# Modulation columns in TensorE column groups, GpSimd low halves at the entry of the down projection, token-order copies placed behind the gates' sigmoids

## The chip, the cores and the metric

The kernel runs on one core of one Trainium2 chip. The metric is the device time of one execution in microseconds (us). The kernel before takes 1423.31 us, the median of 3 runs (1421.92 to 1427.57).

## The reference

One layer over 1024 latent tokens of width 1024, with a prefix of 256 context tokens, in float32:

```
sh1, sc1, g1, sh2, sc2, g2 = split(silu(c) @ mod_w + mod_b, 6)        # one row each, 1024 wide
csh1, csc1, ...            = split(silu(c_ctx) @ mod_w + mod_b, 6)
h  = rmsnorm(x,   norm1_g) * (1 + sc1)  + sh1
hc = rmsnorm(ctx, norm1_g) * (1 + csc1) + csh1
p  = h @ w_in                            # 512 S5 inputs, 3 x 512 short convolution, 2 x 1024 gates
pc = hc @ w_in[:, :512]
y_a = s5_branch(p[:512], pc, ...)        # two directions, state handed from ctx, gelu, then a GLU
y_b = b_gate * conv1d(c_gate * x_val)
merged = sigmoid(p gate_a) * (y_a @ proj_a) + sigmoid(p gate_b) * (y_b @ proj_b)
x  = x + g1 * (merged @ w_out)
h2 = rmsnorm(x, norm2_g) * (1 + sc2) + sh2
a, v = split(depthwise_conv3x3(h2 @ w_up))          # 2 x 2816 channels on a 16 x 64 grid
x  = x + g2 * ((silu(a) * v) @ w_down)
out = rmsnorm(x, final_g)
```

The first two lines are the modulation; the change rewrites how sh1, sc1, csh1 and csc1 are computed.

## The kernel before

Every float32 product of the layer is made of three passes of TensorE over values split into a high half (a rounded copy, written by ScalarE) and a low half (the difference, written by VectorE or GpSimd): `mm3` (L211 to L214) issues high by high, low by high, and high by low. `weight` (L190 to L204) loads 128 rows of a weight and splits them (`whi`, `wlo`); `split` (L206 to L208) does it for an activation.

A tile scheduler sets, at build time, the order of the instructions of each engine from the data dependences, the buffer counts of the pools and its own cost estimates; the engines then take them strictly in that order. `tc.issue_after(ins)` puts what is written inside it behind an instruction. SyncE (SP) and ScalarE (ACT) issue the loads, also in order.

The stages that the change touches, in order of time:

- The start (0 to 62 us). Four tiles of x are loaded and normalised (`norm_rows`: squares summed by ScalarE, a short chain of VectorE operations for the inverse root, four products). For each of 8 slices k of the width, a column of (1 + scale) * norm1_g (`A1`) and one of the shift (`B1`) are needed; `transpose_mod` turns the slice of x, ScalarE applies both columns (`h32a`, L302) and copies the high half (`hhi`, L304), VectorE makes the low half (`hlo`, L307), and `u_pass` multiplies by the slice's w_in rows (`mm_ua`, 12 matmuls per k, accumulated over k). `mod_scale` (L344 to L360) gets the scale columns by TensorE: 8 float32 products with the two condition columns as the stationary operand, a row of two by 128 that ScalarE copies, and a transpose. `mod_shift` (L362 to L374) gets the shift columns by VectorE: a dot product of a 128 x 1024 tile of mod_w transposed with a row of silu(c) that `cond_rows` spread over the partitions by 16 transposes and four copies. `mod_shift` also loads and splits the w_in slice (`wuh`, `wul`, L373).
- The second half of the tokens and the context (63 to 115 us), then the S5 tables, the convolution, the scan and its readouts (to about 400 us), with projections in between. A readout `Zt` goes through memory (`Zd`), and `z` is read back and put into token order by ScalarE (L862). Next to it the gates run: `gate` (L831 to L835) multiplies, then ScalarE's sigmoid (`sggb`) empties the accumulator `mm_gb`.
- The output projection (590 to 700 us): `mixed` (L965 to L971) splits the merged activations into `mh` and `ml`.
- The gated MLP's up projection with its 3 x 3 convolution (700 to 1169 us): `up_conv` (L1047 to L1067). Of the nine taps, ScalarE does the centre and one vertical neighbour (`side`, added by GpSimd, L1056), VectorE does seven (L1064). There are 22 pairs of column tiles; `f[k]` is the product of a pair.
- The down projection in two groups of four token tiles (1169 to 1414 us): `down_operands` (L1092 to L1099) loads w_down's rows and splits `f[k]` into `fhd`, `fld`. In the first group the first four k take token tiles 0 and 1 first, because the accumulators of tiles 2 and 3 are still read by the last convolutions.

Of the kernel before, what the change touches and what calls it, by code (L numbers as in the profile page):

```python
# [42 lines left out]
NAT = KT  # L43
# [113 lines left out]
def layer_kernel(es: ExitStack, tc, I, out):  # L157
# [68 lines left out]
    modx = const.tile([P, 16], F32, name="modx")  # L226
# [35 lines left out]
    mp = pool("mp", bufs=5, stack=es_a)  # L262
# [22 lines left out]
    def norm_rows(xt, ntile, key, dst, tpool, eng, junk=None):  # L285
# [3 lines left out]
        for i in range(ntile):  # L289
            sq = act.activation(junk, xt[i], AF.Square, accum_out=ss[:, i:i + 1])  # L290
# [32 lines left out]
    sc1 = cond_rows(0, mp)
    sx = cond_rows(1, mp)
# [13 lines left out]
    mj = mp.tile([P, D], BF16, name="mj", bufs=1)  # L338

    def mod_dot(mw, s_, dst, junk=mj):  # L340
        dve.tensor_tensor_reduce(out=junk, in0=mw, in1=s_, scale=1.0, scalar=0.0, op0=ALU.mult, op1=ALU.add,
                                 accum_out=dst)

# [880 lines left out]
```

## Time and profile before

| | |
|---|---|
| time, median of 3 runs | 1423.31 us (1421.92 to 1427.57) |
| the profiled execution | 1423.9 us |
| its span, first to last instruction | 1422.0 us |
| granted TensorE clock, mean | 0.997 of full speed |
| busy share: TensorE, VectorE, ScalarE, GpSimd | 97%, 68%, 37%, 29% |
| data moved | 148.71 MB |

The trace has one line for every instruction, in microseconds from the span's start. PE is TensorE's matmuls, PEld its weight loads, DVE is VectorE, ACT is ScalarE, POOL is GpSimd, SP is SyncE. L is the line of the kernel. "out<-in" are the kernel's names; a square bracket at a row's end gives how long the engine stood idle before it, and what ended that. Consecutive instructions of one kind are merged in a row; the duration is then that of all. The duration of a matmul overlaps with the next one's, so the step between two starts is what one costs.

### The profile page before, as it was taken

Reading aid. Unit: us, or ns where it says so; the run is one execution under the profiler, and the core shown is the slowest. Engines: PE = TensorE matmul, PEld = TensorE weight load, DVE = VectorE, ACT = ScalarE, POOL = GpSimd, SP = SyncE. Lnnn points to the kernel's source line nnn. Section 1 sums busy time; section 2 is a strip of 40 time slices with the busy share of each in tenths; the row PEclk is TensorE's granted clock in tenths of the full one; section 3 lists DMA queues with packets and bytes.
Section 4 is the critical chain, followed back from the end, with each engine's and each line's share of the span. In section 5 each row is a group of like instructions: output and inputs, shape, how many; then the busy total and the mean of one; then the engine's idle time right before and its main releaser. Section 6 shows DMA issues by size and latency. Waiting matters only on the chain.

```text
span 1422.0 us, 16940 instructions
## 1 busy us (share of the span) xinstructions
PE 1385.7 (97%) x6488; PEld 1136.4 (80%) x6488; DVE 971.4 (68%) x1464; ACT 528.0 (37%) x749; POOL 406.8 (29%) x183
## 2 busy tenths in 40 slices
PE   7999999999999999999999999999999999999997
PEld 4788887788878888788888888888888887888886
DVE  6866779998336751376487788778878887338655
ACT  5643862212653312244343233332332342324322
POOL 0000000002011133520056545555555465623002
PEclk9999999999999999999999999999999999999999
DMA  9613212512867562242111111111111115433421
GB/s 329 212 54 97 68 60 89 139 52 90 245 219 199 184 203 60 74 148 90 51 60 46 58 45 45 52 52 45 45 58 47 45 59 187 139 102 136 147 90 60
DMA packets 80401, 148.71 MB, mean 105 GB/s; under 512 B 22208, under 2 KB 47040, under 8 KB 80320
## 3 DMA queue, kind: packets, MB, share of 16 engines
q1 hardware_dynamic: 74848, 128.46, 28.9%
q10 hardware_dynamic: 5472, 19.17, 4.0%
q8 instruction: 51, 0.84, 0.2%
q14 instruction: 30, 0.25, 0.1%
HBM read 129.80 MB, written 19.90 MB: 105 GB/s over the span
## 4 chain that ended last, share of the span: by engine, by line
PE 86%; DVE 5%; ACT 3%; DMA 3%; issue 1%; POOL 0%; SPq 0%; ACTq 0%; POOLq 0%; DVEq 0%
PE mm_up L214 11%; PE mm_up L212 11%; PE mm_up L213 11%; PE mm_dn L213 5%; PE mm_dn L212 5%; PE mm_dn L214 5%; PE mm_o L214 2%; PE mm_o L212 2%; PE mm_ga L214 2%; PE mm_o L213 2%; PE mm_ga L213 2%; PE mm_ga L212 2%; PE mm_gb L212 1%; PE mm_gb L213 1%; PE mm_gb L214 1%
## 5 line engine op out<-in xcount | busy, mean ns | idle before, releaser
L1064 DVE SCALAR_TENSOR_TENSOR acc<-mm_up,cw,acc 128x945 f32<-128x945 f32 (+2 forms) x308 | 375.0, 1222 | 100.3 <-POOL acc L1056 91.6
L203 POOL TENSOR_TENSOR wlo<-raw,whi 128x1024 fp32r<-128x1024 f32 x80 | 197.8, 2474 | 705.0 <-ACT whi L200 704.9
L200 ACT ACTIVATE whi<-raw 128x1024 fp32r<-128x1024 f32 x126 | 133.5, 1060 | 530.7 <-issue 165.3
L214 PE MATMUL mm_up<-h2hi,wlo 128*128 128x512 f32 x704 | 273.9, 389 | 0.5 <-POOL wlo L203 0.5
L212 PE MATMUL mm_up<-h2hi,whi 128*128 128x512 f32 x704 | 273.5, 389 | 0.4 <-DVE h2hi L999 0.4
L213 PE MATMUL mm_up<-h2lo,whi 128*128 128x512 f32 x704 | 273.9, 389 | 0.0
L214 PEld LDWEIGHTS mm_up<-h2hi,wlo 128*128 128x128 f32 x704 | 132.1, 188 | 28.3 <-POOL wlo L203 0.9
L212 PEld LDWEIGHTS mm_up<-h2hi,whi 128*128 128x128 f32 x704 | 132.1, 188 | 27.9 <-DVE h2hi L999 0.7
L213 PEld LDWEIGHTS mm_up<-h2lo,whi 128*128 128x128 f32 x704 | 132.1, 188 | 27.7
L213 PE MATMUL mm_dn<-wlo,fhd 128*128 128x512 f32 x308 | 120.1, 390 | 2.5 <-POOL wlo L203 2.5
L212 PE MATMUL mm_dn<-whi,fhd 128*128 128x512 f32 x308 | 118.5, 389 | 1.5 <-DVE acc L1064 1.5
L214 PE MATMUL mm_dn<-whi,fld 128*128 128x512 f32 x308 | 119.9, 389 | 0.0
L1056 POOL TENSOR_TENSOR acc<-acc,side 128x960 f32<-128x960 f32 x44 | 100.4, 2283 | 0.0
L208 DVE TENSOR_TENSOR fld<-f,fhd 128x512 fp32r<-128x512 f32 x44 | 52.8, 1215 | 49.0 <-ACT fhd L207 49.0
L873 DVE CUSTOM_DVE_ANT_0 mw<-mw,sc 128x1024 f32<-128x1024 f32 x32 | 44.1, 1387 | 45.1 <-DMA mw<-in_mod_wT_dram 29.8
L213 PEld LDWEIGHTS mm_dn<-wlo,fhd 128*128 128x128 f32 x308 | 57.8, 188 | 15.3 <-POOL wlo L203 3.5
L212 PEld LDWEIGHTS mm_dn<-whi,fhd 128*128 128x128 f32 x308 | 57.8, 188 | 14.0 <-DVE acc L1064 1.9
L214 PEld LDWEIGHTS mm_dn<-whi,fld 128*128 128x128 f32 x308 | 57.8, 188 | 12.0
L203 DVE TENSOR_TENSOR wlo<-raw,whi 128x1024 fp32r<-128x1024 f32 x46 | 57.0, 1239 | 9.8 <-ACT whi L200 9.8
L1154 POOL TENSOR_TENSOR x1r<-x1r,fgb 128x512 f32<-128x512 f32 x16 | 21.7, 1362 | 129.6 <-ACT fjk L1153 129.6
L1075 POOL TENSOR_TENSOR f<-f,acc 128x1024 f32<-128x1024 f32 x22 | 53.3, 2424 | 10.0 <-DVE acc L1064 10.0
L197 DVE TENSOR_TENSOR raw<-raw,g2b 128x1024 f32<-128x1024 f32 x22 | 28.4, 1289 | 38.1 <-DMA raw<-in_ffn_w_down_dram 38.1
(325 smaller groups left out, 2667.1 us busy)
## 6 DMA issues: line engine op xcount, KB each, us to landing
raw<-in_ffn_w_up_dram SPq DMA_DIRECT2D x44, 512.0 KB
raw<-in_ffn_w_down_dram SPq DMA_DIRECT2D x44, 512.0 KB
mw<-in_mod_wT_dram SPq DMA_DIRECT2D x32, 512.0 KB
raw<-in_w_in_dram SPq DMA_DIRECT2D x17, 512.0 KB
wt<-Yd SPq DMA_DIRECT2D x16, 384.0 KB
raw<-in_w_in_dram ACTq DMA_DIRECT2D x11, 512.0 KB
mt<-in_mod_wT_dram SPq DMA_DIRECT2D x8, 512.0 KB
mn<-in_mod_nat_dram SPq DMA_DIRECT2D x8, 512.0 KB
```

The source lines that it names most:

```text
L197: dve.tensor_tensor(raw, raw, scale, op=ALU.mult)
L200: act.activation(hi, raw, AF.Copy)
L203: (lo_eng or dve).tensor_tensor(lo, raw, hi.bitcast(F32), op=ALU.subtract)
L208: return dve.tensor_tensor(lo, src, hi.bitcast(F32), op=ALU.subtract)
L212: pe.matmul(ps, lh, rh, start=first, stop=False)
L213: pe.matmul(ps, lh, rl, start=False, stop=False)
L214: pe.matmul(ps, ll, rh, start=False, stop=last)
L873: dve.tensor_tensor_reduce(out=mw, in0=mw, in1=sc2, scale=1.0, scalar=0.0, op0=ALU.mult, op1=ALU.add, accum_out=modc[:, n:n + 1])
L1056: pool_e.tensor_tensor(acc[:, 1:, :], acc[:, 1:, :], side[:, 1:, :], op=ALU.add)
L1064: dve.scalar_tensor_tensor(acc[:, r0:r1, c0:c1], u[:, r0 + dr:r1 + dr, c0 + dc:c1 + dc], cw[:, m, i:i + 1], acc[:, r0:r1, c0:c1], op0=ALU. ...
L1075: pool_e.tensor_tensor(f[k], f[k], v, op=ALU.mult)
L1154: pool_e.tensor_tensor(xt[i][:, sl], xt[i][:, sl], fgb[:, sl], op=ALU.mult)
```

## The change

- `mod_cols1` replaces `mod_scale` and the dots of `mod_shift`. All 16 column tiles (8 of shift, 8 of scale) go to TensorE. The two condition columns are padded with zeros to 32 (`condp`), and the eight partial products of a tile are written to four groups of 32 rows of the accumulator, two accumulated in each. ScalarE copies the 128 x 256 result of a k, and a product with a 0/1 matrix of two columns (`sel`) sums the four groups and turns the row into a column. ScalarE then writes `A1` and `B1` from the accumulator. `cond_rows`, its 16 transposes and four copies are gone, and so are the 16 dots.
- `load_wu` keeps the load and split of the w_in slice. The pool of modulation tiles has 7 buffers in place of 5; the tiles are the same size and number.
- The squares of x tiles 1 and 3 move from ScalarE to VectorE.
- The loads of the four readout tiles `zj` are written ahead of the modulation's, and the copies to token order (`z_tokens`) are to be issued behind a gate's sigmoid. silu(c) for the later modulation columns is a sigmoid by ScalarE and a product by VectorE.
- `mh` has three buffers in place of two.
- The last pair of the up projection takes its side tap on VectorE: no `side` copy and no GpSimd addition.
- The low halves of `f[0]` to `f[5]` for the first down group are made by GpSimd, behind the low half of the weight of that k.
- The deferred products of token tiles 2 and 3 are ordered by tile, then by k.

The diff, cut to its core:

```diff
--- before.py
+++ after.py
@@ -40,7 +40,7 @@
-NAT = KT
+NAT = 2 * KT
...
         with held("dve") if lo_eng is None else nullcontext():
-            (lo_eng or dve).tensor_tensor(lo, raw, hi.bitcast(F32), op=ALU.subtract)
+            hold["lo"] = (lo_eng or dve).tensor_tensor(lo, raw, hi.bitcast(F32), op=ALU.subtract)
         return hi, lo
 
-    def split(hi, lo, src):
+    def split(hi, lo, src, eng=None):
         act.activation(hi, src, AF.Copy)
-        return dve.tensor_tensor(lo, src, hi.bitcast(F32), op=ALU.subtract)
+        return (eng or dve).tensor_tensor(lo, src, hi.bitcast(F32), op=ALU.subtract)
 
     def mm3(ps, lhs, rhs, first, last):
         (lh, ll), (rh, rl) = lhs, rhs
...
-    mp = pool("mp", bufs=5, stack=es_a)
+    mp = pool("mp", bufs=7, stack=es_a)
...
-            sq = act.activation(junk, xt[i], AF.Square, accum_out=ss[:, i:i + 1])
+            if key == "a" and i % 2:
+                dve.tensor_tensor_reduce(out=tpool.tile([P, D], BF16, name=f"jd_{key}{i}", tag="h32"), in0=xt[i], in1=xt[i],
+                                         scale=1.0, scalar=0.0, op0=ALU.mult, op1=ALU.add, accum_out=ss[:, i:i + 1])
+            else:
+                sq = act.activation(junk, xt[i], AF.Square, accum_out=ss[:, i:i + 1])
...
-    act.activation(cond, cond, AF.Silu)
-
-
-    def cond_rows(i, mpool):
-        t = mpool.tile([P, D], F32, name=f"cr{i}", bufs=1)
-        for n in range(2):
-            ps = ax_tile([P, HALF], f"cr{i}_{n}")
-            for k in range(4):
-                pe.transpose(ps[:, k * P:(k + 1) * P], cond[:, 4 * n + k, i:i + 1].to_broadcast([P, P]), ident)
-            act.activation(t[:, n * HALF:(n + 1) * HALF], ps, AF.Copy)
-        return t
-
-    sc1 = cond_rows(0, mp)
-    sx = cond_rows(1, mp)
+    condp = mp.tile([P, KT, 32], F32, name="condp", bufs=1)
+    dve.memset(condp, 0.0)
+    act.activation(condp[:, :, 0:2], cond, AF.Silu)
+    sel = mp.tile([P, 2], F32, name="sel", bufs=1)
+    dve.tensor_tensor(sel, ident[:, 0:2], ident[:, 32:34], op=ALU.add)
+    for j in (64, 96):
+        dve.tensor_tensor(sel, sel, ident[:, j:j + 2], op=ALU.add)
+    modb1 = mp.tile([P, KT], F32, name="modb1", bufs=1)
+    dve.scalar_tensor_tensor(modb1, modb[:, KT:2 * KT], 1.0, n1g, op0=ALU.add, op1=ALU.mult)
...
-    def mod_scale(k):
-        n = KT + k
-        mw = mp.tile([P, D], F32, name=f"mn{k}", tag="mw")
-        dma[k] = sync.dma_start(mw, I["mod_nat"][k])
-        pr = prp.tile([P, P + 2], F32, name=f"pr{k}", tag="pr")
-        row, col = pr[0:2, :P], pr[:, P:]
-        for q in range(KT):
-            pe.matmul(row, cond[:, q, :], mw[:, q * P:(q + 1) * P], start=(q == 0), stop=(q == KT - 1))
-        rw = mp.tile([2, P], F32, name=f"rw{k}", tag="rw", bufs=1)
-        act.activation(rw, row, AF.Copy)
-        pe.transpose(col, rw, ident[0:2, 0:2])
-        dve.tensor_tensor(A1[:, :, k], col, modb[:, n:n + 1].to_broadcast([P, 2]), op=ALU.add)
-        dve.scalar_tensor_tensor(A1[:, :, k], A1[:, :, k], 1.0, n1g[:, k:k + 1].to_broadcast([P, 2]),
-                                 op0=ALU.add, op1=ALU.mult)
-
-    def mod_shift(k):
-        mw = mp.tile([P, D], F32, name=f"mt{k}", tag="mw")
-        sync.dma_start(mw, I["mod_wT"][k * P:(k + 1) * P, :])
+    def mod_cols1(k):
+
+
+        pr = prp.tile([P, 2 * P + 4], F32, name=f"pr{k}", tag="pr")
+        rows = pr[:, :2 * P].rearrange("p (c n) -> p c n", c=2)
+        cols = pr[:, 2 * P:].rearrange("p (c i) -> p c i", c=2)
+        for c in range(2):
+            mw = mp.tile([P, D], F32, name=f"m{c}_{k}", tag="mw")
+            dma[k] = sync.dma_start(mw, I["mod_nat"][c * KT + k])
+            for s_ in range(2):
+                for j in range(4):
+                    q = 4 * s_ + j
+                    pe.matmul(rows[32 * j:32 * j + 32, c, :], condp[:, q, :], mw[:, q * P:(q + 1) * P],
+                              start=(s_ == 0), stop=(s_ == 1))
+        rw = mp.tile([P, 2, P], F32, name=f"rw{k}", tag="rw", bufs=1)
+        act.activation(rw, rows, AF.Copy)
+        for c in range(2):
+            pe.matmul(cols[:, c, :], rw[:, c, :], sel, start=True, stop=True)
+        act.activation(B1[:, :, k], cols[:, 0, :], AF.Identity, bias=modb[:, k:k + 1])
+        act.activation(A1[:, :, k], cols[:, 1, :], AF.Identity, scale=n1g[:, k:k + 1], bias=modb1[:, k:k + 1])
+
+    def load_wu(k):
         raw = wp.tile([P, D], F32, name=f"wuraw{k}", tag="raw")
         junk[k] = raw[:, SW:].bitcast(BF16)
         sync.dma_start(raw[:, :SW].rearrange("p (m n) -> p m n", m=MS),
                        I["w_in"][0:MS].rearrange("m p (k n) -> k p m n", k=KT)[k])
         act.activation(wuh[k], raw[:, :SW], AF.Copy)
         with held("dve"):
-            mod_dot(mw, sc1, modc[:, k:k + 1])
-            dve.tensor_tensor(B1[:, 0, k:k + 1], modc[:, k:k + 1], modb[:, k:k + 1], op=ALU.add)
             dve.tensor_tensor(wul[k], raw[:, :SW], wuh[k].bitcast(F32), op=ALU.subtract)
-            mod_dot(mw, sx, modx[:, k:k + 1])
...
-    mod_shift(0)
     for k in range(NE):
-        mod_scale(k)
-    mod_shift(1)
+        mod_cols1(k)
+        load_wu(k)
     half_a(0)
     for k in range(KT):
-        if k + 2 < KT:
-            if k + 2 >= NE:
-                mod_scale(k + 2)
-            mod_shift(k + 2)
-        if k + 2 == XB:
+        if k + NE < KT:
+            mod_cols1(k + NE)
+            load_wu(k + NE)
+        if k + NE == XB:
...
-    dve.tensor_tensor(B1[:, 1, :], modx[:, :KT], modb[:, :KT], op=ALU.add)
...
-        act.activation(sg, psg, AF.Sigmoid)
+        hold["sig"] = act.activation(sg, psg, AF.Sigmoid)
...
+    zj = []
     for m in range(MS):
-        zj = zp.tile([P, L, NCL], F32, name=f"zj{m}", tag="zj", bufs=2)
-        sync.dma_start(zj, Zd[m])
-        act.activation(z[m].rearrange("p (c j) -> p j c", j=L), zj, AF.Copy)
+        zj.append(zp.tile([P, L, NCL], F32, name=f"zj{m}", tag="zj", bufs=2))
+        sync.dma_start(zj[m], Zd[m])
+
+    def z_tokens(m):
+
+        with tc.issue_after(hold["sig"].ins):
+            act.activation(z[m].rearrange("p (c j) -> p j c", j=L), zj[m], AF.Copy)
+
     es_md = ExitStack()
     md = pool("md", bufs=2, stack=es_md, side="right")
     sc2 = md.tile([P, D], F32, name="sc2", bufs=1)
     sync.dma_start(sc2, I["c"].partition_broadcast(P))
-    act.activation(sc2, sc2, AF.Silu)
+    sg2 = md.tile([P, D], F32, name="sg2", tag="mw")
+    act.activation(sg2, sc2, AF.Sigmoid)
+    dve.tensor_tensor(sc2, sc2, sg2, op=ALU.mult)
...
+        for m in {MA + 1: (0, 1), MA + 2: (2, 3)}.get(d, ()):
+            z_tokens(m)
...
-        hi = wo.tile([P, MA, P], F32R, name=f"mh{t}_{j}", tag="mh", bufs=2)
+        hi = wo.tile([P, MA, P], F32R, name=f"mh{t}_{j}", tag="mh", bufs=3)
...
-        side = kp.tile([P, ROWS, GW], F32, name=f"side{m}", tag="side")
         act.activation(acc, u, AF.Copy, scale=cw[:, m, 4:5])
-        act.activation(side[:, 1:, :], u[:, :ROWS - 1, :], AF.Copy, scale=cw[:, m, 1:2])
-        pool_e.tensor_tensor(acc[:, 1:, :], acc[:, 1:, :], side[:, 1:, :], op=ALU.add)
+        aside = m % KF < KF - 1
+        if aside:
+            side = kp.tile([P, ROWS, GW], F32, name=f"side{m}", tag="side")
+            act.activation(side[:, 1:, :], u[:, :ROWS - 1, :], AF.Copy, scale=cw[:, m, 1:2])
+            pool_e.tensor_tensor(acc[:, 1:, :], acc[:, 1:, :], side[:, 1:, :], op=ALU.add)
         for dr in (-1, 0, 1):
             for dc in (-1, 0, 1):
-                if dc == 0 and dr < 1:
+                if dc == 0 and (dr == 0 or dr < 0 and aside):
...
-        split(fh, fl, f[k][:, c0:c0 + NG * P])
+        start = c0 == 0 and 0 <= k < 6
+        with tc.issue_after(hold["lo"].ins) if start else nullcontext():
+            split(fh, fl, f[k][:, c0:c0 + NG * P], pool_e if start else None)
...
-                    for kk in range(EDGE):
-                        for i in range(2, NG):
+                    for i in range(2, NG):
+                        for kk in range(EDGE):
...
```

The first place is the start on TensorE. Before, the rows are the spreading of the condition (`ax_cr`), the scale products (`pr`, from a tile `mn`), the transposes of x (`ax_ta`):

```order
L319 MATMUL ax_cr_0_192<-ident,packed 128x128 x4
L319 MATMUL ax_cr_1_198<-ident,packed 128x128 x4
L319 MATMUL ax_cr_0_205<-ident,packed 128x128 x4
L319 MATMUL ax_cr_1_211<-ident,packed 128x128 x4
L354 MATMUL pr_257<-mn_255,packed 2x128 x8
L354 MATMUL pr_273<-mn_271,packed 2x128 x8
L300 MATMUL ax_ta_296<-ident,xa_182 128x128
```

And now, where `m_0` and `m_1` are the shift and scale tiles of k = 0 and 1, and L357 is the sum of the groups:

```order
L352 MATMUL pr_228<-m_0_229,condp 32x128 x8
L352 MATMUL pr_228<-m_0_239,condp 32x128 x8
L357 MATMUL pr_228<-sel,rw_249 128x2 x2
L303 MATMUL ax_ta_290<-ident,xa_181 128x128
L303 MATMUL ax_ta_330<-ident,xa_181 128x128
L352 MATMUL pr_259<-m_1_260,condp 32x128 x8
L303 MATMUL ax_ta_290<-ident,xa_183 128x128
L303 MATMUL ax_ta_330<-ident,xa_183 128x128
L303 MATMUL ax_ta_290<-ident,xa_185 128x128
L303 MATMUL ax_ta_330<-ident,xa_185 128x128
L352 MATMUL pr_259<-m_1_270,condp 32x128 x8
```

The 16 transposes of the condition are gone, and each k has two groups of eight products with 32 rows out, where it had one with 2. On VectorE the 16 dots (two per k) no longer stand between the low halves.

The second place is ScalarE at the seventh gate (`sggb`). Before, with the readout copies `z` and the silu of c (`sc`):

```order
L862 ACTIVATE z_3446<-zj_3450 128x8x128
L862 ACTIVATE z_3447<-zj_3453 128x8x128
L867 ACT_TABLE_LOAD
L867 ACTIVATE sc_3465<-sc_3465 128x1024
L200 ACTIVATE whi_3749<-raw_3747 128x1024
L834 ACT_TABLE_LOAD
L834 ACTIVATE sggb_3707<-mm_gb_3658 128x1024
L862 ACTIVATE z_3448<-zj_3456 128x8x128
```

And now:

```order
L858 ACTIVATE z_3475<-zj_3479 128x8x128
L858 ACTIVATE z_3476<-zj_3481 128x8x128
L865 ACT_TABLE_LOAD
L865 ACTIVATE sg_3492<-sc_3490 128x1024
L200 ACTIVATE whi_3780<-raw_3778 128x1024
L825 ACTIVATE sggb_3736<-mm_gb_3687 128x1024
L858 ACTIVATE z_3477<-zj_3483 128x8x128
L858 ACTIVATE z_3478<-zj_3485 128x8x128
```

The copies of tiles 0 and 1 still stand ahead of this gate's sigmoid; one of the two table loads between them is gone. On SP the loads of `zj` 2 and 3 now stand ahead of the first two modulation tiles `mw`, where they stood behind them.

The third place is the entry of the down projection on VectorE before, with the low halves (`fld`) and the convolution of column tile 21 (`acc_8761`):

```order
L1064 SCALAR_TENSOR_TENSOR acc_8662<-mm_up_8613,cw,acc_8662 128x960
L208 TENSOR_TENSOR fld_0_8843<-f_5859,fhd_0_8842 128x512
L1064 SCALAR_TENSOR_TENSOR acc_8662<-mm_up_8613,cw,acc_8662 128x15x63
L208 TENSOR_TENSOR fld_1_8865<-f_5860,fhd_1_8864 128x512
L208 TENSOR_TENSOR fld_2_8887<-f_5861,fhd_2_8886 128x512
L208 TENSOR_TENSOR fld_3_8909<-f_5862,fhd_3_8908 128x512
L208 TENSOR_TENSOR fld_4_8979<-f_5863,fhd_4_8978 128x512
L208 TENSOR_TENSOR fld_5_9013<-f_5864,fhd_5_9012 128x512
L1064 SCALAR_TENSOR_TENSOR acc_8761<-mm_up_8681,cw,acc_8761 128x15x63 x2
```

And GpSimd now, from the second weight's low half on:

```order
L203 TENSOR_TENSOR wlo_8897<-raw_8893,whi_8895 128x1024
L1078 TENSOR_TENSOR f_5910<-f_5910,acc_8693 128x1024
L203 TENSOR_TENSOR wlo_8875<-raw_8871,whi_8873 128x1024
L208 TENSOR_TENSOR fld_0_8870<-f_5890,fhd_0_8869 128x512
L208 TENSOR_TENSOR fld_1_8892<-f_5891,fhd_1_8891 128x512
L203 TENSOR_TENSOR wlo_8919<-raw_8915,whi_8917 128x1024
L208 TENSOR_TENSOR fld_2_8914<-f_5892,fhd_2_8913 128x512
L203 TENSOR_TENSOR wlo_8941<-raw_8937,whi_8939 128x1024
L208 TENSOR_TENSOR fld_3_8936<-f_5893,fhd_3_8935 128x512
L203 TENSOR_TENSOR wlo_9011<-raw_9007,whi_9009 128x1024
L208 TENSOR_TENSOR fld_4_9006<-f_5894,fhd_4_9005 128x512
```

The six low halves stand in GpSimd's queue in place of the two `side` additions, and on VectorE the convolutions of the last pair follow those of the pair before directly.

## Rows read from the trace of the kernel before

**Rows 1.** Waits of TensorE: operation, waited for, us in total, times, longest.

```profile
PE mm_gb L212 <- ACT sggb L834: 3.4, 1, 3.4
PE mm_dn L213 <- POOL wlo L203: 2.5, 2, 2.0
...
PE mm_dn L212 <- DVE acc L1064: 1.5, 1, 1.5
...
PE mm_o L214 <- DVE ml L208: 1.1, 1, 1.1
```

**Rows 2.** Busy us of PE, PEld, DVE, ACT, POOL by stretch; granted clock, DMA share, GB/s.

```profile
30.00:40.00 10.00, 10.00 (x61) 7.07 (x61) 9.24 (x37) 7.33 (x13) 0.00 (x0) 1.00 1.00 372
40.00:50.00 10.00, 10.00 (x60) 7.37 (x59) 8.75 (x47) 5.12 (x11) 0.00 (x0) 1.00 0.56 201
...
418.00:422.00 4.00, 4.00 (x11) 3.12 (x12) 3.26 (x5) 3.87 (x2) 0.08 (x1) 0.61 0.91 292
```

**Rows 3.** Timeline of TensorE, start to 62 us: start, duration, instruction, [idle before].

```profile
7.58 2.89 PE L319 MATMUL ax_cr<-ident,packed 128*128 128x128 f32 x12 [7.58 <-ACT packed L311]
...
18.58 0.22 PE L357 MATMUL pr<-ident,rw 2*128 2x2 f32 x1
...
26.50 0.73 PE L212 MATMUL mm_ua<-hhi,wuh 128*128 128x512 f32 x2
...
44.21 1.91 PE L354 MATMUL pr<-mn,packed 128*2 128x128 f32 x16
46.05 0.73 PE L212 MATMUL mm_ua<-hhi,wuh 128*128 128x512 f32 x2
...
61.58 0.40 PE L213 MATMUL mm_ua<-hlo,wuh 128*128 128x512 f32 x1
61.81 0.40 PE L214 MATMUL mm_ua<-hhi,wul 128*128 128x512 f32 x1
```

**Rows 4.** Timeline of VectorE and ScalarE in the start; then the dots' line.

```profile
12.38 0.17 DVE L134 TENSOR_SCALAR rm_a<-ss_a 128x4 f32<-128x4 f32 x1 [6.47 <-ACT jk_a L290]
...
22.51 1.45 ACT L302 ACTIVATE h32a<-ax_ta,B,A 128x512 f32<-128x512 f32 x2 [3.41 <-DVE A L359]
...
L341 DVE CUSTOM_DVE_ANT_0 mj<-mt,cr x16: 1212/1219/1224, 17.2 to 52.3; 128x1024 bf16<-128x1024 f32 x16
```

**Rows 5.** Timeline at 170 us: products in four column groups (L660).

```profile
170.01 0.39 PE L213 MATMUL mm_x<-hlo,whi 128*128 128x512 f32 x1
...
170.33 0.40 PEld L660 LDWEIGHTS ax_K<-W,Bk 128*32 128x32 f32 x16 [0.35 <-issue]
170.33 0.66 PE L660 MATMUL ax_K<-W,Bk 128*32 128x128 f32 x16
170.93 0.20 PEld L511 LDWEIGHTS ax_w<-ident,T 128*128 128x128 f32 x2 [0.20 <-issue]
```

**Rows 6.** Timeline of ScalarE at the seventh gate.

```profile
408.05 4.19 ACT L862 ACTIVATE z<-zj 128x1024 f32<-128x1024 f32 x2 [9.11 <-DMA zj<-Zd]
412.26 1.28 ACT L867 ACT_TABLE_LOAD   x1
...
415.58 1.28 ACT L834 ACT_TABLE_LOAD   x1
416.88 1.02 ACT L834 ACTIVATE sggb<-mm_gb 128x1024 f32<-128x1024 f32 x1
```

**Rows 7.** Timeline at the down projection's entry: VectorE, GpSimd; then GpSimd's line 1154.

```profile
1160.97 0.69 DVE L208 TENSOR_TENSOR fld<-f,fhd 128x512 fp32r<-128x512 f32 x1 [0.43 <-ACT fhd L207]
...
1162.69 13.33 DVE L208 TENSOR_TENSOR fld<-f,fhd 128x512 fp32r<-128x512 f32 x5
1175.95 16.67 DVE L1064 SCALAR_TENSOR_TENSOR acc<-mm_up,cw,acc 128x945 f32<-128x945 f32 x14
...
1178.12 4.71 POOL L203 TENSOR_TENSOR wlo<-raw,whi 128x1024 fp32r<-128x1024 f32 x2
...
L1154 POOL TENSOR_TENSOR x1r<-x1r,fgb x16: 1263/1296/2135, 1279.7 to 1414.9; 128x512 f32<-128x512 f32 x16
```

More of the change, by code (lines that the diff above doesn't have):

```diff
@@ L225, in layer_kernel @@
     modc = const.tile([P, 48], F32, name="modc")
-    modx = const.tile([P, 16], F32, name="modx")
     A1 = const.tile([P, 2, KT], F32, name="A1")
@@ L335, in half_tiles @@
         return [t[m // 2][:, (m % 2) * HALF:(m % 2 + 1) * HALF] for m in range(MS)]
[L338 to L342, printed above, removed]
     psa = half_tiles([mm_tile(f"ua{i}") for i in range(2)])
     dma, junk = {}, {}
-    def mod_scale(k):
-        n = KT + k
-        mw = mp.tile([P, D], F32, name=f"mn{k}", tag="mw")
-        dma[k] = sync.dma_start(mw, I["mod_nat"][k])
-        pr = prp.tile([P, P + 2], F32, name=f"pr{k}", tag="pr")
-        row, col = pr[0:2, :P], pr[:, P:]
-        for q in range(KT):
-            pe.matmul(row, cond[:, q, :], mw[:, q * P:(q + 1) * P], start=(q == 0), stop=(q == KT - 1))
-        rw = mp.tile([2, P], F32, name=f"rw{k}", tag="rw", bufs=1)
-        act.activation(rw, row, AF.Copy)
-        pe.transpose(col, rw, ident[0:2, 0:2])
-        dve.tensor_tensor(A1[:, :, k], col, modb[:, n:n + 1].to_broadcast([P, 2]), op=ALU.add)
-        dve.scalar_tensor_tensor(A1[:, :, k], A1[:, :, k], 1.0, n1g[:, k:k + 1].to_broadcast([P, 2]),
-                                 op0=ALU.add, op1=ALU.mult)
@@ L1187, in layout @@
     a["mod_wT"] = A["mod_w"][0].T
-    a["mod_nat"] = A["mod_w"][0][:, D:D + NAT * P].reshape(KT, P, NAT, P).transpose(2, 1, 0, 3).reshape(NAT, P, D)
+    a["mod_nat"] = A["mod_w"][0][:, :NAT * P].reshape(KT, P, NAT, P).transpose(2, 1, 0, 3).reshape(NAT, P, D)
     a["norm2_g"] = _cols(A["norm2_g"][0])
```

## The prediction

> **What bounds the kernel now.** The table says TensorE works for 97% of the span, so a faster neighbour is worth only what TensorE waits for, plus TensorE work that goes. I read the list of waits by engine first. In [rows 1] four waits belong to places that the change touches: 3.4 us at the seventh gate, 2.5 and 1.5 us at the entry of the down projection, 1.1 us in the output projection. Then the timeline of the start. TensorE issues nothing for 7.58 us, then spreads the condition by 16 transposes, and the first product of a layer matrix starts only at 26.50 [rows 3]. The stage's last starts at 61.81, 0.23 us after the one before it [rows 3], and TensorE is busy without a gap in 30 to 50 us [rows 2]. What holds 26.50 back is a chain: ScalarE's `h32a` stood idle 3.41 us for VectorE's `A` [rows 4], and VectorE was then in the dots (16 of 1.22 us, from 17.2 to 52.3 us, in [rows 4]). DMA is full to 40 us (share 1.00) and at 0.56 after it [rows 2].
>
> **The change part by part.** The sum is made against the profiled execution's 1423.9 us, which is 0.6 above the median of 1423.3.
>
> **Start, TensorE's work.** Removed: 16 transposes at 2.89 / 12 = 0.24, so 3.9 us; 8 bursts of scale products, each 46.05 - 44.21 = 1.84, so 14.7; 8 small transposes of 0.22, so 1.8 [rows 3]. Together 20.4 us. Added: 16 bursts in column groups. The kernel has such a burst once, at 170 us: the matmul before it starts at 170.01 and takes one step of 0.23, the next weight load starts at 170.93, so a burst of 16 instructions holds the engine 0.69 us [rows 5]. 16 of them are 11.0 us, and 16 sums of groups at the 0.22 of the small transpose are 3.5: 14.5 us. TensorE has 5.9 us less to do.
>
> Around such a burst the weight loads stood idle 0.35 and 0.20 us "for issue" [rows 5]. The Trainium skill, "TensorEngine Tiling (Array Packing)", section Tiling Modes, says that a change of tiling mode drains TensorE, which speaks against 16 short bursts among full-width products. By that rule and by the row the price is the same, because the 0.69 us holds both gaps.
>
> **Start, the chain.** VectorE loses 16 x 1.22 = 19.5 us and gets two sums of squares, at the dot's price 2.4. The squares end about 2 us sooner (VectorE's chain starts at 12.38 now [rows 4]; two of four squares and four copies leave ScalarE). `A` and `B` come from ScalarE directly, without the dots ahead. Following the queues by hand, the first `u_pass` starts near 19 us in place of 26.5. This is not all won: the w_in slices stand behind the modulation tiles on SP while DMA is full, their buffer has two places, and VectorE's order puts some 45 small operations of the S5 tables ahead of the third low half. The hand chain puts the passes at 19, 29, 34, 42, 48, 51, 54 and the end at 57 to 58 us, against 62.0. I take 4.5 us. Bounds: nothing, if slices and small operations hold the last pass where it is; 8 us, which is where TensorE's own work ends (start 10, 96 matmuls x 0.23 = 22.1, 14.5 for the columns, some 5 of transposes, 2 of filling: 54). Only TensorE's idle time pays for this; from here on the queues keep their order up to the gates, so I let the shift through.
>
> **The gate.** ScalarE holds the gate's accumulator until its sigmoid at 416.88; ahead stand two `z` copies (408.05, 4.19 us, which came 9.11 us after anything else because the data landed late) and two table loads of 1.28 [rows 6]. By the order, the copies of tiles 0 and 1 are still ahead of this sigmoid, so that the change does not do for this gate what it says is included here; one table load goes: 1.28. The loads of `zj` 0 and 1 no longer share DMA with two modulation tiles, worth 0 to 2 us; I take 0.3. After the wait the granted clock was 0.61 over 418 to 422 [rows 2], a mix of the 1.2 and the 2.4 GHz level, after 3.4 us of idling: 4 x 0.39 = 1.6 us. With a wait of about 1.8 us I expect the clock to hold. Sum 3.2; bounds 1.3 (clock falls all the same, nothing lands sooner) and 4.9. The modulation dots of this stage start later, as SP now loads `zj` 2 and 3 first; the same bytes are moved, so they end about where they did, and if they end 3 us later the low halves of `z` behind them on VectorE are late and TensorE pays what is left over, up to 2 us. So the lower bound is -0.7.
>
> **Output projection.** The third `mh` buffer lets ScalarE write a high half sooner; the low half waits for VectorE as before, and `ml` keeps two buffers. Of the 1.1 us [rows 1] I take 0.6, bounds -0.5 and 1.1.
>
> **Down projection's entry.** Five low halves took VectorE 13.33 us, 2.67 each, beside GpSimd's, where one alone took 0.69; only at 1175.95 do the last pair's convolutions begin, 14 in 16.67 us, 1.19 each, and GpSimd's low halves in that time were 4.71 / 2 = 2.36 each [rows 7]. Moved to GpSimd, six low halves of 128 x 512 cost 1.30 each (median of line 1154, the same shape [rows 7]), 7.8 us, and two side additions over a whole column tile leave its queue. VectorE starts the 16 convolutions (14, plus two side taps) near 1166.5 and ends 16 x 1.19 = 19 us later at 1185.5, where it now ends at 1192.6. GpSimd's chain, at 2.36 and 1.30, delivers the first four pairs by 1169, 1172, 1175 and 1179; TensorE consumes two token tiles of a k in 12 x 0.23 = 2.8 us from 1169, so it waits a few tenths in all. Tile 2's accumulator is free at 1181, tile 3's at 1185.5, and the new order of the deferred products asks for tile 3 only 24 x 0.23 = 5.5 us after tile 2. The waits are 2.5 + 1.5 us [rows 1], counted from the end of a matmul of 0.40 whose successor would have started 0.23 after it [rows 3]; with 0.17 more for each of the three they are 4.5, and 0.5 remain: 4.0. Bounds: 0 (GpSimd becomes the bound) and 4.5. If this cover is gone, each low half adds up to 1.30 us per k to TensorE's wait, 5 us for four.
>
> VectorE and GpSimd slow each other in these rows (2.67 against 0.69). The Trainium skill, "Perfetto Trace Analysis", section Optimizing Scalar/DVE Operations, says that the two share a read port and that moving work between them might not help. By that rule the sum would lose this term; the rows that bear on it are the convolutions, 1.19 us each with GpSimd busy or idle, and GpSimd's 2.36 beside them. It is the third rival below.
>
> Sum: 4.5 + 3.2 + 0.6 + 4.0 = 12.3; 1423.9 - 12.3 = 1411.6, or 1411 against the median.
>
> **The rivals.** (1) The start gives nothing: DMA full to 40 us, the slices last on SP and the small operations keep the last `u_pass` at 61.8, or a stage behind it takes the gain back (VectorE is at 9.2 and 8.8 of 10 us in 30 to 50 [rows 2]). For it: those rows. Against: 17 us leave VectorE just there. Price: 12.3 - 4.5 = 7.8, so 1415.5. (2) The column groups run one after the other, at the two-column price: 16 x 1.84 + 3.5 = 32.9 us of TensorE for 20.4, 12.5 more in a stage that TensorE ends, for 4.5 less: 1423.3 + 12.5 - 7.8 = 1428, slower. It decides from 1.3 us a burst on (20.4 - 3.5 = 16.9 over 16 is 1.06 at which TensorE's work breaks even, and the chain's slack of some 4 us adds 0.25). Against: 0.69 at line 660, whose products are 128 wide too [rows 5], in float32 as here. (3) The two engines' low halves are no better on GpSimd: the entry gives 0, and 12.3 - 4.0 = 8.3 leaves 1415. Against: two additions leave the queue that gets the 7.8 us. (4) The start gives its upper bound, 8: 1407.5.
>
> **How the numbers follow.** Chances: forecast 0.56 (own range 1407 to 1414.5), rival 1 0.17, rival 3 0.08, rival 4 0.13, rival 2 and other losses 0.06. 0.5%, about what a measurement here tells from no change, is 7.1 us: faster is below 1416.2, slower above 1430.4. The forecast, rival 4, and a little over half of rivals 1 and 3, whose times stand just inside, give 0.56 + 0.13 + 0.14 = 0.83, less some for a stage that I follow wrongly: 0.8; slower 0.03, same 0.17. The range takes in rivals 1, 3 and 4 with 3 us around them, and leaves out rival 2: 1404 to 1419.
>
> **What would show it.** In the trace after: bursts of L352 of 0.7 us, not 1.8; no wait of ScalarE for `A`; the first `mm_ua` near 19 and the last near 57 us; one table load between the `z` copies and the gate's sigmoid, a wait there of about 2 us and a granted clock of 1.00 behind it; at the entry no low half of 2.7 us on VectorE, convolutions from 1166 minus the shift, and waits of TensorE under 1 us together. The prediction is wrong if the last `mm_ua` stays at 62 us, or if the stages between 62 and 400 us take longer than now by what the start gave.

## The result, and the profile after

The changed kernel takes 1414.9 us (median of 6 runs, 1413.6 to 1419.3) against 1422.8 for the kernel before (6 runs): a ratio of 0.9943, 95% interval 0.9925 to 0.9962. A second sample of the same kernel later gave 1414.8 (0.9946, 0.9927 to 0.9964). It is faster by 7.9 us where 12.3 were forecast; the time lies inside the range, just above the forecast's own range.

The profiled execution took 1417.0 us with a span of 1415.2, 6.8 less than before. TensorE's waits in it (operation, waited for, us in total, times, longest):

```profile
PE pr L352 <- DMA m<-in_mod_nat_dram: 10.0, 2, 9.8
PE mm_x L212 <- DVE cx L695: 2.4, 1, 2.4
PE mm_glu L214 <- DVE wlo L203: 1.8, 2, 1.0
...
PE mm_pa L214 <- DVE wlo L203: 1.1, 1, 1.1
PE mm_gb L214 <- POOL wlo L203: 0.9, 1, 0.9
PE mm_gb L212 <- ACT sggb L825: 0.8, 1, 0.8
...
PE mm_o L214 <- DVE ml L208: 0.6, 1, 0.6
...
PE mm_dn L214 <- POOL fld L208: 0.4, 1, 0.4
```

The gate's 3.4, the entry's 2.5 and 1.5 and the output projection's 1.1 [rows 1] are now 0.8, 0.4 and 0.6. New are waits of the GLU and of proj_a (`mm_glu`, `mm_pa`) for low halves from VectorE, and one of the gate for GpSimd.

How far the changed kernel is ahead at marks of the two traces (start time before less start time after, both read from the lines of one tile):

| mark | before | after | ahead |
|---|---|---|---|
| first `mm_x` (convolution inputs) | 117.6 | 112.8 | 4.8 |
| last `mm_x` | 263.5 | 260.2 | 3.3 |
| last `ax_Y` (readouts) | 396.4 | 392.8 | 3.6 |
| first `mm_ga`, behind the gates' stretch | 436.2 | 429.6 | 6.6 |
| first `mm_pa`, behind the GLU | 480.3 | 476.2 | 4.1 |
| last `mm_pa` | 590.9 | 588.3 | 2.6 |
| last `mm_o` | 686.9 | 683.7 | 3.2 |
| last `mm_up` | 1168.7 | 1165.8 | 2.9 |
| last `mm_dn` | 1407.6 | 1400.7 | 6.9 |

So in this pair of traces the start (4.8), the gates (3.0), the output projection (0.6) and the entry (4.0) gave what was forecast within 0.3 us each, and 5.5 us net went in stages that the forecast let through: 1.5 between the two `mm_x` marks, 2.5 at the GLU, 1.5 up to the last `mm_pa`. The experiments show how much of this is chance of the two executions.

The start: column groups, sums and the first layer products on TensorE (start, duration, instruction, [idle before]):

```profile
9.81 1.08 PE L352 MATMUL pr<-m,condp 128*32 128x128 f32 x16 [9.81 <-DMA m<-in_mod_nat_dram]
...
21.73 1.20 PE L212 MATMUL mm_ua<-hhi,wuh 128*128 128x512 f32 x2
...
28.90 0.64 PE L352 MATMUL pr<-m,condp 128*32 128x128 f32 x16
```

A burst lasts 0.64, about as at line 660 (0.66 [rows 5]), but 1.08 up to about 23 us: TensorE, idle until 9.81, worked at half rate there (as at its lower level of 1.2 GHz, by the durations). The clock column of 10 to 20 us reads 1.00, but that is no reading: the trace's record of the granted clock begins only at 23.3 us. The first layer product starts at 21.73, where 19 was forecast, against 26.50 [rows 3].

The stretch behind the wait of 2.4 us for `cx`, after which `mm_x` goes on at 210.4 (length, busy us of PE, PEld, DVE, ACT, POOL; granted clock, DMA share, GB/s):

```profile
211.00:215.00 4.00, 4.00 (x12) 3.18 (x11) 3.97 (x6) 0.76 (x1) 0.00 (x0) 0.57 0.24 48
```

The clock fell there (4 x 0.43 = 1.7 us), which it did not in the trace of before, whose wait at this place was as long (2.4 us, `mm_x` goes on at 215.3):

```profile
216.00:220.00 4.00, 4.00 (x19) 3.29 (x19) 3.96 (x6) 0.62 (x1) 0.00 (x0) 1.00 0.24 67
```

The gate on ScalarE, and VectorE from the first modulation dot to the GLU's low half:

```profile
403.35 4.18 ACT L858 ACTIVATE z<-zj 128x1024 f32<-128x1024 f32 x2 [7.98 <-DMA zj<-Zd]
407.54 1.28 ACT L865 ACT_TABLE_LOAD   x1
...
410.75 1.00 ACT L825 ACTIVATE sggb<-mm_gb 128x1024 f32<-128x1024 f32 x1
```

```profile
409.93 1.23 DVE L866 TENSOR_TENSOR sc<-sc,sg 128x1024 f32<-128x1024 f32 x1 [14.16 <-ACT sg L865]
412.42 2.05 DVE L872 CUSTOM_DVE_ANT_0 mw<-mw,sc 128x1024 f32<-128x1024 f32 x1 [1.27 <-DMA mw<-in_mod_wT_dram]
...
434.92 0.17 DVE L912 TENSOR_TENSOR modc<-modc,modk 128x8 f32<-128x8 f32 x1
...
440.75 1.22 DVE L203 TENSOR_TENSOR wlo<-raw,whi 128x1024 fp32r<-128x1024 f32 x1
```

One table load is gone and the copies came sooner, as the prediction said (403.35 against 408.05, of which 3.6 is the lead up to the last `ax_Y`). But the eight dots end (`modc`) at 434.92, 5.3 us after TensorE's first `mm_ga` at 429.6; TensorE wants the `wlo` behind them at 441.1 and gets it at 441.97. Before, they ended at the same time, and that was 0.9 ahead of the first `mm_ga` at 436.2:

```profile
435.27 0.17 DVE L911 TENSOR_TENSOR modc<-modc,modk 128x8 f32<-128x8 f32 x1
```

The entry of the down projection, on VectorE and GpSimd, is to be read beside [rows 7]:

```profile
1163.54 18.94 DVE L1067 SCALAR_TENSOR_TENSOR acc<-mm_up,cw,acc 128x945 f32<-128x945 f32 x16 [4.68 <-ACT acc L1054]
...
1166.11 2.56 POOL L208 TENSOR_TENSOR fld<-f,fhd 128x512 fp32r<-128x512 f32 x2
```

A low half costs GpSimd 1.28, the 16 convolutions 1.18 each, side by side; they end at 1182.5, 16.5 us behind the first `mm_dn` (1166.0); 16.6 was forecast (1185.5 behind 1168.95).

### The profile page after: what moved, and what is told of

The parts are those of the page before. It is cut to its first block, busy times and chain, and to the rows that moved or that the text cites. A ratio compares the mean times of both kernels' runs of the same rounds, so it can differ in the third digit from the quotient of the medians.

```text
span 1415.2 us, 17172 instructions
## 1 busy us (share of the span) xinstructions
PE 1382.3 (98%) x6624; PEld 1135.0 (80%) x6624; DVE 943.0 (67%) x1413; ACT 524.4 (37%) x754; POOL 407.3 (29%) x187
## 4 chain that ended last, share of the span: by engine, by line
PE 82%; DMA 6%; DVE 5%; ACT 3%; issue 2%; POOL 1%; SPq 0%; DVEq 0%; ACTq 0%; POOLq 0%
PE mm_up L212 11%; PE mm_up L214 11%; PE mm_up L213 11%; PE mm_dn L214 5%; PE mm_dn L213 5%; PE mm_dn L212 5%; DMA mw<-in_mod_wT_dram 4%; PE mm_o L214 2%; PE mm_o L212 2%; PE mm_o L213 2%; PE mm_gb L212 1%; PE mm_gb L213 1%; PE mm_gb L214 1%; DVE mw L872 1%; PE mm_ga L214 1%
## 5 line engine op out<-in xcount | busy, mean ns | idle before, releaser
L1059 POOL TENSOR_TENSOR acc<-acc,side 128x960 f32<-128x960 f32 x42 | 94.9, 2260 | 0.0
L208 DVE TENSOR_TENSOR fld<-f,fhd 128x512 fp32r<-128x512 f32 x38 | 36.8, 977 | 53.9 <-ACT fhd L207 53.9
L214 PEld LDWEIGHTS mm_dn<-whi,fld 128*128 128x128 f32 x308 | 57.8, 188 | 13.1 <-POOL fld L208 1.3
L213 PEld LDWEIGHTS mm_dn<-wlo,fhd 128*128 128x128 f32 x308 | 57.8, 188 | 12.1
L212 PEld LDWEIGHTS mm_dn<-whi,fhd 128*128 128x128 f32 x308 | 57.8, 188 | 12.0
```

The source lines that it names most:

```text
L208: return (eng or dve).tensor_tensor(lo, src, hi.bitcast(F32), op=ALU.subtract)
L212: pe.matmul(ps, lh, rh, start=first, stop=False)
L213: pe.matmul(ps, lh, rl, start=False, stop=False)
L214: pe.matmul(ps, ll, rh, start=False, stop=last)
L1059: pool_e.tensor_tensor(acc[:, 1:, :], acc[:, 1:, :], side[:, 1:, :], op=ALU.add)
```

## The experiments

Ratios are against runs of the kernel before that were taken beside each group of kernels. For the first four it took 1422.5 us.

**front_only**: the kernel before with the start's edits alone.

> The kernel before with the start's edits alone (columns by TensorE in column groups, squares shared, no spreading of the condition); gates, output projection and down projection as before. Theory (the start gives 5 us and nothing behind it eats it by itself): the last mm_ua ends near 57 to 60 us, the last mm_uc 5 us sooner than before, 1417 to 1418.5 us. Rival (the middle takes up what the start gives, so the changed kernel's gain is the gates and the entry): 1421 to 1423 us. A granted clock near 0.6 behind the 2.4 us wait at the first mm_x of the second stretch would cost 1.6 us of it in that execution.

1417.0 us, ratio 0.9953 (0.9935 to 0.9972). In its trace it is 7.2 us ahead at the first `mm_x`, 5.6 at the last (the clock fell between them), 7.7 at the last `mm_dn`. The start gives over 5 us by itself and the stages behind it do not take it up.

**lows_on_dve**:

```diff
-        start = c0 == 0 and 0 <= k < 6
+        start = False
```

> The changed kernel with the six low halves of the entry on VectorE again, all else as changed (the last pair still has no side addition). Theory (the entry is worth 4.0 us and the low halves are what holds it): waits of 2 to 4 us at the first mm_dn come back, low halves of 2.7 us on VectorE, time 2 to 4 us above the changed kernel, 1417 to 1419 us. Rival (the missing side additions alone did it): within 1 us of the changed kernel.

1420.2 us, 0.9978 (0.9964 to 0.9992), 5.3 above the changed kernel, more than expected. VectorE, TensorE, and the stretch with the clock:

```profile
1154.91 11.26 DVE L208 TENSOR_TENSOR fld<-f,fhd 128x512 fp32r<-128x512 f32 x5
1166.10 18.92 DVE L1067 SCALAR_TENSOR_TENSOR acc<-mm_up,cw,acc 128x945 f32<-128x945 f32 x16
```

```profile
1180.17 0.50 PE L212 MATMUL mm_dn<-whi,fhd 128*128 128x512 f32 x1 [4.00 <-DVE acc L1067]
```

```profile
1180.00:1184.00 4.00, 3.83 (x12) 3.04 (x13) 3.89 (x5) 1.06 (x1) 0.00 (x0) 0.69 0.02 4
```

With the low halves on VectorE the last pair's two more taps only lengthen its queue, and behind the wait of 4.0 the clock is down (0.69). The low halves on GpSimd hold the entry's gain; without them, leaving out the side additions loses: from the last `mm_up` to the last `mm_dn` this kernel takes 240.7 us, the kernel before 238.9, the changed one 234.9.

**glu_lows_pool**:

```diff
-            wt = weight(I["glu_w"][m // 2])
+            wt = weight(I["glu_w"][m // 2], pool_e)
...
-            wt = weight(I["proj_a"][d // 2])
+            wt = weight(I["proj_a"][d // 2], pool_e)
```

> The changed kernel with the low halves of the GLU's and of proj_a's weights on GpSimd, where VectorE made them behind modulation dots that wait for their loads. Theory (the dots, paced by their loads, hold the low halves back, which is where 2.5 and 1.3 us of the gain were lost): no mm_glu or mm_pa wait for a low half, 2.5 to 4 us faster than the changed kernel, 1411 to 1412.5 us. Rival (TensorE only meets the next late thing there, the z or sgz chain): under 1 us.

1419.1 us, 0.9977 (0.9960 to 0.9993): 4 us slower than the changed kernel. No `mm_glu` wait, but at 530 us proj_a's low half stood in GpSimd's queue ahead of a gate's:

```profile
534.48 0.79 PE L214 MATMUL mm_ga<-hhi,wlo 128*128 128x512 f32 x1 [4.36 <-POOL wlo L203]
```

The wait was moved, not removed; the expectation failed.

**mw_before_zj** gives the sigmoid of c a buffer of its own, by which SP loads two modulation tiles ahead of `zj` 2 and 3 again:

```diff
-    sg2 = md.tile([P, D], F32, name="sg2", tag="mw")
+    sg2 = zp.tile([P, D], F32, name="sg2", tag="sgz", bufs=1)
```

> The changed kernel with the sigmoid of c in a buffer of its own: the order of every engine is as in the changed kernel but for the loads on SP, where the first two modulation tiles stand ahead of zj 2 and 3 again. Theory (the late start of the dots' loads makes them late for the GLU): dots end 1 to 3 us sooner, the mm_glu waits of 0.9 and 1.0 shrink, 0 to 2 us faster, 1413 to 1415 us; the z copies land later and the gate's wait grows by up to 2 us. Rival (the loads are paced by DMA and two buffers whatever their first place): dots end at the same time, no difference.

1415.0 us, 0.9933 (0.9909 to 0.9956); TensorE waits 2.4 us at the GLU. The loads' first place is not the cause. That the dots would end sooner was a miss: they end at 433.1, which is 6.9 us behind the first `mm_ga` of this trace (5.3 in the changed kernel).

Beside the next four the kernel before took 1422.1 us.

**changed_again**: the changed kernel, unaltered.

> The changed kernel unaltered, for its spread. Theory (the trace of the changed kernel met a start at half rate for longer, 23.6 against about 17.8 us in the four traces with the same start, and this is chance): the last mm_ua starts near 57.5 and the last mm_uc near 107 us, time about 1415 with single executions 2 to 4 us apart. Rival (this program starts so every time): 59.9 and 109.3 us again.

1414.8 us, single runs 1411.5 to 1416.8. The last `mm_ua` starts at 57.8, the last `mm_uc` (the context's products) at 107.2: that the slow start lasted so long in the first trace is chance. TensorE's rate doubles at another time in this execution, 18.4 us in place of 23.3.

**mw_first_glu_pool**: `mw_before_zj` with the GLU's low halves on GpSimd and proj_a's left on VectorE.

> The changed kernel with the sigmoid of c in a buffer of its own (two modulation tiles ahead of zj 2 and 3 on SP) and with the low halves of the GLU's weights alone on GpSimd; proj_a's stay on VectorE, since GpSimd's queue made TensorE wait 4.4 us with them. Theory (the GLU's low halves behind the dots cost 1.8 to 4 us with the clock): no mm_glu wait, no 4.4 us mm_ga wait, 1411 to 1413 us, 2 to 4 us below the changed kernel. Rival (the wait moves on to proj_a or the gates): 1414 to 1416 us.

1414.3 us, 0.9947 (0.9931 to 0.9964). No `mm_glu` wait; proj_a's became 1.5. No gain that can be told: the rival was right.

**no_token_order**: the changed kernel with the readout loads, copies and silu of c as before.

> The changed kernel with the readout loads, z copies and the silu of c as before; start, output projection and entry as changed. Theory (what this part gives at the gate, 2.9 us in the profile, it gives back at the GLU): the gate waits 2.2 us or more again, no mm_glu wait, 1413 to 1416 us, within 1.5 us of the changed kernel. The prediction's own term (3.2 us for the gate): 1418 us.

1410.4 us, 0.9919 (0.9902 to 0.9936): 4.4 faster than the changed kernel beside it (1414.8), faster than either side expected. In its trace it is 10.3 us ahead at the first `mm_ga` and 10.2 at the first `mm_pa`; nothing is lost at the GLU.

**serial_columns**: all eight products in one group.

```diff
-                    pe.matmul(rows[32 * j:32 * j + 32, c, :], condp[:, q, :], mw[:, q * P:(q + 1) * P],
-                              start=(s_ == 0), stop=(s_ == 1))
+                    pe.matmul(rows[0:32, c, :], condp[:, q, :], mw[:, q * P:(q + 1) * P],
+                              start=(q == 0), stop=(q == KT - 1))
```

> The changed kernel with all eight partial products of a modulation tile in one group of 32 columns, one after the other, in place of four groups side by side; the sum takes 32 rows. Theory (four groups run side by side, 0.65 against 1.84 us a burst): bursts of 1.8 us, 16 x 1.2 = 19 us more TensorE work in the start, of which some hides in the wait for the loads, last mm_ua 10 to 18 us later, 1426 to 1434 us. Rival (the groups were serial, the bursts are short for another reason): bursts of 0.65 us and the changed kernel's time.

1434.4 us, 1.0085 (1.0070 to 1.0101), the last `mm_ua` at 73.7, 16 us later than in changed_again. Eighteen steps of its products:

```profile
20.32 2.15 PE L352 MATMUL pr<-m,condp 128*32 128x128 f32 x18
```

0.12 us each, 1.9 a burst of 16, against 0.64: four groups do run side by side. This is rival 2, at 19.6 us over the changed kernel rather than 17.

Beside the last ones the kernel before took 1424.1 us.

**silu_kept**: the changed kernel with one operation for the silu. Its instructions stand on every engine as in no_token_order: the new order of `zj` and `z_tokens` moves nothing, so all that this part of the change does is the sigmoid and the product.

```diff
-    sg2 = md.tile([P, D], F32, name="sg2", tag="mw")
-    act.activation(sg2, sc2, AF.Sigmoid)
-    dve.tensor_tensor(sc2, sc2, sg2, op=ALU.mult)
+    act.activation(sc2, sc2, AF.Silu)
```

> The changed kernel with the silu of c as one ScalarE operation again, and nothing else: the readout loads and z copies stay as changed. On every engine its instructions then stand as in no_token_order; against mw_before_zj there is one table load more on ScalarE and one product less on VectorE. Theory (of the whole part on the readouts only this product of sc and sg moves anything, by starting the dots later): as no_token_order, 1409 to 1412 us, first dot right behind the silu, no mm_glu wait. Rival (the 4 us between those two runs were spread): 1413 to 1416 us.

1410.1 us, 0.9906 (0.9885 to 0.9927). **sigmoid_own_buffer**, the same kernel as mw_before_zj, is the sigmoid and product beside it:

> The same kernel as mw_before_zj, on the same chip as silu_kept: sigmoid and product, in a buffer of its own. Theory: 1414 to 1416 us, 3 to 5 us above silu_kept, with mm_glu waiting for a low half. Rival: within 1 us of silu_kept.

1412.8 us, 0.9924 (0.9903 to 0.9946): 2.7 more, a little under the expected 3 to 5. GpSimd's low half (one line) and VectorE in silu_kept, then in sigmoid_own_buffer, from the first dot to the end of the eight:

```profile
406.51 2.40 POOL L203 TENSOR_TENSOR wlo<-raw,whi 128x1024 fp32r<-128x1024 f32 x1 [11.67 <-ACT whi L200]
405.46 1.23 DVE L870 CUSTOM_DVE_ANT_0 mw<-mw,sc 128x1024 f32<-128x1024 f32 x1 [12.70 <-ACT sc L864]
406.61 3.38 DVE L870 CUSTOM_DVE_ANT_0 mw<-mw,sc 128x1024 f32<-128x1024 f32 x1
...
410.28 1.22 DVE L870 CUSTOM_DVE_ANT_0 mw<-mw,sc 128x1024 f32<-128x1024 f32 x1 [0.27 <-DMA mw<-in_mod_wT_dram]
...
425.77 0.17 DVE L910 TENSOR_TENSOR modc<-modc,modk 128x8 f32<-128x8 f32 x1
```

```profile
406.00 2.45 POOL L203 TENSOR_TENSOR wlo<-raw,whi 128x1024 fp32r<-128x1024 f32 x1 [10.33 <-ACT whi L200]
404.94 1.23 DVE L866 TENSOR_TENSOR sc<-sc,sg 128x1024 f32<-128x1024 f32 x1 [11.36 <-DMA mw<-in_mod_wT_dram]
406.20 3.32 DVE L872 CUSTOM_DVE_ANT_0 mw<-mw,sc 128x1024 f32<-128x1024 f32 x1
...
414.69 1.23 DVE L872 CUSTOM_DVE_ANT_0 mw<-mw,sc 128x1024 f32<-128x1024 f32 x1 [4.01 <-DMA mw<-in_mod_wT_dram]
...
430.78 0.17 DVE L912 TENSOR_TENSOR modc<-modc,modk 128x8 f32<-128x8 f32 x1
```

In both, the dot that meets GpSimd's low half takes 3.3. With the silu that is the second dot, and the first has freed its buffer at 406.6; with the product it is the first, so the third tile's load starts 3 us later and its dot stands at 414.69, not 410.28. The eight dots end 5 us later, and the GLU's low half behind them, for which TensorE now waits:

```profile
437.83 0.50 PE L214 MATMUL mm_glu<-zh,wlo 128*128 128x512 f32 x1 [1.13 <-DVE wlo L203]
```

The delay is in every trace: with the product ahead, 23.8 to 26.6 us pass from it to the end of the eight dots (eight traces); with one silu, 20.3 to 21.0 from the first dot (six traces). That the dot's meeting with GpSimd is the whole of it is not shown: in the changed kernel the first dot took 2.05, not 3.3, in glu_lows_pool 1.22, and the eight took 25.0 and 23.8 us there.

**warm_start**: no_token_order with 20 unused transposes of the identity ahead.

> no_token_order with 20 transposes of the identity by TensorE ahead of its first product, their result unused; the other engines' orders are unchanged. Theory (the first 8 us of TensorE's work in the start run at half rate because the engine idled until 9.8 us): bursts of 0.65 us from 10 us on, last mm_ua 1 to 4 us sooner, 1406 to 1410 us. Rival (the loads and small operations hold the start anyway): within 1 us of no_token_order, 1410 us.

1409.7 us, 0.9908 (0.9882 to 0.9934): no difference that can be told from silu_kept beside it (1410.1), which has the orders of no_token_order. The transposes ended at 5.9, and TensorE was at half rate when the first tile landed:

```profile
9.77 1.08 PE L356 MATMUL pr<-m,condp 128*32 128x128 f32 x16 [3.89 <-DMA m<-in_mod_nat_dram]
```

The transposes themselves ran at half rate: 0.421 us each, where the transposes of x, of the same shape, take 0.273 in most places (name, lines: shortest, median, longest in ns):

```profile
L327 PE MATMUL ax_warm<-ident x20: 421/421/475, 1.4 to 5.5; 128*128 128x128 f32 x20
L303 PE MATMUL ax_ta<-ident,xa x32: 272/273/477, 13.7 to 43.8; 128*128 128x128 f32 x32
```

The trace's record of the clock begins at 6.3 us with full speed, when the transposes were over, and has the half from 9.8 to 23.4, after 3.9 us of idling. So this run does not show what a start at full rate would be worth. The stretches of 6 to 10 and of 10 to 20 us, with the columns as above:

```profile
6.00:10.00 4.00, 0.23 (x7) 0.26 (x10) 2.49 (x5) 2.37 (x4) 0.00 (x0) 0.97 1.03 422
10.00:20.00 10.00, 9.13 (x100) 5.94 (x96) 8.98 (x36) 3.83 (x8) 0.00 (x0) 0.50 1.06 384
```

**before_again**: the kernel before, unaltered, executed once.

> The kernel before, unaltered, for a second trace. Theory (each of the eight traces with the new start shows a lower clock behind the 2.4 us wait at 210 us, the one of before does not, and this hangs on when the wait falls and not on the change): either outcome at 215 us; the start as in the first trace, last mm_ua near 61.8 and last mm_uc near 114.7 us. Rival (the new start itself brings the dip): clock 1.00 there again.

1420.7 us. At the seventh gate this execution of the kernel before waits 1.0, not 3.4, and its clock falls at 216 us:

```profile
PE mm_gb L212 <- ACT sggb L834: 1.0, 1, 1.0
```

```profile
216.00:220.00 4.00, 4.00 (x13) 3.16 (x13) 3.97 (x6) 1.06 (x2) 0.00 (x0) 0.67 0.17 36
```

So the dip there does not come from the new start, and the gate's long wait was that of one execution out of two. From the last `ax_Y` to the first `mm_ga`, where the forecast put its gate term, this execution takes 35.7 us, the first one 39.8, the changed kernel 36.8.

## Why the prediction was right or wrong

- **Start, 4.5 us: mechanism right, a little small.** The bursts last 0.64 and not 1.84, and the side-by-side groups are what does it (serial_columns). In eight further traces with this start the first `mm_ua` stands at 19.6 to 20.5 and the last at 57.2 to 58.0 (in one more at 21.7 and 59.9 again), which is the hand chain's 19 and 57 to 58. But the last `mm_ua` is not the whole price: from it to the first `mm_x` TensorE took 55.8 us before (55.2 in before_again) and now takes 52.9, a gain that the forecast left out. One product and four transposes that now stand ahead of the last `mm_ua`, about 0.7, and a wait of `mm_ub` for ScalarE of 0.5 are part of it; the rest was not traced. At the first `mm_x` the gain is 6.7 to 7.5 in the eight traces; front_only measured 5.6 for the whole. The first trace's 4.8 there, so near 4.5, is luck: 1.9 up to the last `mm_ua`, held back by the half rate, and 2.9 behind it. The forecast has the half rate nowhere: it took the removed transposes at 0.24, where products of the same size step by 0.115 at 44 us (1.84 / 16), and the added bursts at 0.69, where the first six of the changed kernel's trace last 1.08.
- **The gate, 3.2 us: the step that failed.** Two parts of it. The wait of 3.4 with the lower clock behind it was the profiled execution's; with the old order at this gate other traces wait 1.0 (before_again, at full clock), 2.2 (front_only) and 0.3 (no_token_order), so there was less to win. And "the same bytes are moved, so they end about where they did" took the dots' end alone: they do end at the same time (434.92 and 435.27), but TensorE comes 6.6 us sooner and wants the low half behind them. What keeps them back is the product of `sc` and `sg` on VectorE, which the sum left out; they are paced by two buffers, and where a dot waited for its load in the two traces above, 3.6 to 5.2 us passed from the freeing of its buffer to its start. The bound named for this, -0.7 us, was too mild: with everything else of the change in place, the sigmoid and product cost 2.7 to 4.4 us net (silu_kept and no_token_order against their neighbours). The SP order that the prediction feared is not it (mw_before_zj), and to take the GLU's wait away alone gains nothing (mw_first_glu_pool).
- **Output projection, 0.6: right in this pair, not tested by itself.** 1.1 became 0.6 in the waits, and the marks gained 0.6; but before_again, with two `mh` buffers, does not show the wait either, and takes 95.1 us from the last `mm_pa` to the last `mm_o` where the first trace took 96.0 and the changed kernel takes 95.4.
- **Entry, 4.0: right in size and mechanism** (lows_on_dve): 2.9 to 6.9 in the marks, one wait of 0.4 left. The new order of the deferred products does nothing: with it undone, every engine's order is the same as in the changed kernel.
- **The rivals.** 1 (the start eaten) fell by front_only; 3 (GpSimd no better) by lows_on_dve; 2 (groups serial) by serial_columns, at the price worked out within 3 us. The measured 1414.9 is the time of rivals 1 and 3 (1415.5 and 1415), but neither is its cause.
- **The sum** came out inside the range partly because two misses went opposite ways. no_token_order, which has every part but the gate's, is 11.7 us below the kernel before, where those parts were forecast at 4.5 + 0.6 + 4.0 = 9.1; the gate's part, forecast at 3.2 to the good, then costs 4.4.

The changed kernel less its sigmoid and product, 1410.1 us, beats both kernels.

## What to carry to other kernels

When a stage is sped up ahead of a chain that loads pace, ask what in an in-order queue stands behind that chain: here a weight's low half stood behind dots with two buffers, and a product of 1.2 us ahead of the first dot cost 2.7 to 4.4. A stall seen in one trace is worth its mean over executions; a second trace of the kernel before would have cut the gate's term. Of an edit that is to reorder, compare the built order first: two of this change's edits moved nothing.

## What the runs showed of the hardware

- Column groups of 32 run side by side: 0.64 us for 16 instructions, 1.9 in one group.
- TensorE's rate after an idle start was low until 18.4 us in one trace of the changed kernel and 23.3 us in another, worth 2 us at the first `mm_x` (110.7 and 112.8). Twenty transposes from 1.4 to 5.9 us did not change that: they ran at half rate themselves, the clock read 0.97 over 6 to 10 us, and with TensorE idle for 3.9 us it read 0.50 over 10 to 20 us, with the same bursts of 1.08.
- Where the record of the clock has not begun, the clock column says nothing: it reads 1.00 over 10 to 20 us of the changed kernel's trace, whose bursts last 1.08.
- After the same wait of 2.4 us at one place, the clock fell in one trace of the kernel before (0.67) and stayed at 1.00 in the other. From the first to the last `mm_x` the trace at 1.00 takes 145.9 us, the other 147.3. With the new start, silu_kept kept 1.00 (145.8) and the others that have this wait took 147.4 to 147.5.
- A dot of VectorE with both operands in SBUF took 3.3 beside GpSimd's subtraction and 1.23 without it; convolutions of VectorE that read one operand from the accumulator and one from SBUF took 1.18 beside such a subtraction.
